# Softmax over rows of 512: VectorE's and ScalarE's work in blocks of eight rows in place of four

## The chip, the cores and the metric

The kernel runs on one core of one Trainium2 chip. The metric is the device time of one execution in microseconds (us), as the median over several runs. The kernel before the change took 163.42 us (median of 10 runs, 162.94 to 163.77).

Four engines of the core appear in this kernel. VectorE (DVE in the profile) and ScalarE (ACT) compute. SyncE (SP) only starts loads. GpSimd (POOL) writes four constants at the start and does nothing else. Beside them, sixteen DMA engines move data between the HBM (the chip's main memory) and the SBUF (the core's working memory of 128 partitions). Each engine runs its own list of instructions in order, and waits on semaphores where it needs another engine's result or a transfer.

## The reference

The input is 16 x 1024 rows of 512 float32 numbers, 33.55 MB. Every row is divided by 0.5, and the softmax is taken over it:

```python
temp = 0.5
x_scaled = x / temp
x_max = np.max(x_scaled, axis=-1, keepdims=True)
exp_x = np.exp(x_scaled - x_max)
return (exp_x / np.sum(exp_x, axis=-1, keepdims=True)).astype(np.float32)
```

The output has the size of the input, so 67.1 MB have to be moved in all.

## The kernel before

The 16384 rows are cut into eight tiles of 2048 rows. Each of the 128 partitions holds G = 16 consecutive rows of a tile, which is 32 KB a partition and 4 MB a tile. The pool of tiles has six buffers (`data`, `bufs=6`), and the whole computation is done in place: a tile is loaded, each row in it is replaced by its exponentials and then by the scaled result, and the tile is stored from where it lies. So the loads of the first six tiles wait for nothing, and the loads of tiles 6 and 7 wait until tiles 0 and 1 have been stored.

A tile is loaded with one DMA, issued by SyncE (line 59); only tile 0 is loaded in two, its first four rows and then its other twelve, so that the work can begin early. A tile is stored with one DMA of 4 MB, issued from ScalarE's instruction list (line 102).

The computation goes by blocks of B = 4 rows a partition, so four blocks a tile and 32 in all. Four functions handle a block:

- `shift` runs on VectorE. One reduction (line 65) takes the negated maximum of all four rows of the block, and one small multiplication (line 67) doubles it, because the input's scaling by 1 / 0.5 is folded into the exponential. The result is called `bias`.
- `exponentials` runs on ScalarE. One instruction a row (line 74) computes exp(2x + bias) and its sum over the row. In the trace it shows as two entries, the activation and a short reading of the accumulator.
- `scale_vector` runs on VectorE. One reciprocal of the block's sums (line 87), and then one multiplication a row for three of the four rows (line 89).
- `scale_scalar` runs on ScalarE: the fourth row is multiplied by its reciprocal there, with one copy instruction with a scale (line 95).

The order on every engine is written out by hand in a loop over the blocks (lines 104 to 116). Iteration i issues, in this order, the load of a tile (when block i is the first of one), `shift(i)` and `exponentials(i)`, then `scale_vector(i - 1)`, `scale_scalar(i - 2)` and `store(i - 3)`. A store is issued only when block i - 3 was the last of its tile. So the store of a tile stands on ScalarE's list three blocks behind the tile's last one: behind the exponentials of the third block of the next tile, and behind one scaled copy. For the last tile, the three iterations after the last block finish what is left.

The words "iteration" and "block" are used in this sense below; a block is written (tile, first row), so (7, 8) is the third block of the last tile.

Of the kernel before, what the change touches and what calls it, by code (L numbers as in the profile page):

```python
# [1 line left out]

# [4 lines left out]


@with_exitstack
def kernel(  # L10
    ctx: ExitStack,
    tc: tile.TileContext,
    x: bass.AP,
    out: bass.AP,
):
    nc = tc.nc
    fp32 = mybir.dt.float32
    P = nc.NUM_PARTITIONS
    AX = mybir.AxisListType.X
    EXP = mybir.ActivationFunctionType.Exp  # L20
    COPY = mybir.ActivationFunctionType.Copy
    MAX = mybir.AluOpType.max

    D = x.shape[-1]
    xf = x.flatten_outer_dims()
    of = out.flatten_outer_dims()
    N = xf.shape[0]

    G = 16
    B = 4
    N_ACT = 1
    C = N // (P * G)
    assert C * P * G == N
    xr = xf.rearrange("(c p g) d -> c p g d", p=P, g=G)
    outr = of.rearrange("(c p g) d -> c p g d", p=P, g=G)

    FIRST = [(0, 4), (4, 16)]  # L40

    data = ctx.enter_context(tc.tile_pool(name="data", bufs=6))
    stats = ctx.enter_context(tc.tile_pool(name="stats", bufs=6))

    ctx.enter_context(tc.manual_schedule())


    warm = stats.tile([P, 1], fp32, name="warm", bufs=1)
    nc.vector.memset(warm, 0.0)  # L49
    nc.scalar.activation(out=warm, in_=warm, func=EXP)  # L50

    tiles = {}
    blocks = [(c, b) for c in range(C) for b in range(0, G, B)]
    state = {}

    def load(c):
        xt = tiles[c] = data.tile([P, G, D], fp32, name="xt")
        for lo, hi in FIRST if c == 0 else [(0, G)]:
            nc.sync.dma_start(out=xt[:, lo:hi, :], in_=xr[c][:, lo:hi, :])  # L59

    def shift(i):
        c, b = blocks[i]
        xb = tiles[c][:, b : b + B, :]
        negmax = stats.tile([P, B], fp32, name="negmax")
        nc.vector.tensor_reduce(negmax, xb, axis=AX, op=MAX, negate=True)  # L65
        bias = stats.tile([P, B], fp32, name="bias")
        nc.vector.tensor_scalar_mul(bias, negmax, 2.0)  # L67
        state[i] = (xb, bias)

    def exponentials(i):  # L70
        xb, bias = state[i]
        sums = stats.tile([P, B], fp32, name="sums")
        for g in range(B):
            nc.scalar.activation(  # L74
                out=xb[:, g, :],
                in_=xb[:, g, :],
                func=EXP,
                bias=bias[:, g : g + 1],
                scale=2.0,
                accum_out=sums[:, g : g + 1],  # L80
            )
        state[i] = (xb, sums)

    def scale_vector(i):
        xb, sums = state[i]
        recip = stats.tile([P, B], fp32, name="recip")
        nc.vector.reciprocal(recip, sums)  # L87
        for g in range(B - N_ACT):
            nc.vector.tensor_scalar_mul(xb[:, g, :], xb[:, g, :], recip[:, g : g + 1])  # L89
        state[i] = (xb, recip)  # L90

    def scale_scalar(i):
        xb, recip = state[i]
        for g in range(B - N_ACT, B):
            nc.scalar.activation(  # L95
                out=xb[:, g, :], in_=xb[:, g, :], func=COPY, scale=recip[:, g : g + 1]
            )

    def store(i):
        c, b = blocks[i]  # L100
        if b + B == G:
            nc.scalar.dma_start(out=outr[c], in_=tiles[c])

    n = len(blocks)
    for i in range(n + 3):
        if i < n:
            if blocks[i][1] == 0:
                load(blocks[i][0])
            shift(i)
            exponentials(i)  # L110
        if 1 <= i <= n:
            scale_vector(i - 1)
        if 2 <= i <= n + 1:
            scale_scalar(i - 2)
        if 3 <= i:
            store(i - 3)


# [1 line left out]
_INS = ['x']  # L120
_OUTS = [((16, 1024, 512), 'float32')]


# [23 lines left out]
```

## Time and profile before

| what | value |
|---|---|
| median of 10 runs | 163.42 us |
| the profiled execution's own time | 163.34 us |
| span from its first to its last instruction | 161.4 us |
| VectorE busy | 119.7 us, 74% of the span |
| ScalarE busy | 114.8 us, 71% of the span |
| moved by DMA | 67.14 MB, 416 GB/s over the span |

The profiled execution's time is 1.94 us longer than its span; that difference lies outside of what the instructions show. The profile calls an instruction by its line and by the tile that it writes and reads. In a line of the timeline, the first two numbers are the start and the duration in us, and the bracket at the end tells how long the engine had been idle and what ended that. The names ACTq and SPq stand for the sequencers of ScalarE and SyncE, which issue DMAs without keeping the engine itself busy. In the table of windows, the columns are the window and its length, then the busy time and the number of instructions of each engine, the clock of TensorE (which is not used here), the share of time that the DMA engines were busy, and the data rate in GB/s.

### The profile page before, as it was taken

The numbers are of one execution on the slowest core, as the hardware profiler recorded it, in microseconds if no ns is written. First come the engines' busy times: TensorE is split into PE (matmuls) and PEld (weight loads), VectorE is DVE, ScalarE is ACT, GpSimd is POOL, SyncE is SP. The second block draws the span as 40 slices with busy tenths as digits, with TensorE's granted clock in tenths as the row PEclk, the third lists the DMA queues.
The fourth block names the chain that finished last, engine by engine and source line by source line (L and its number), as shares of the span: only waits on it lengthen the run. The fifth ranks groups of instructions, "written<-read, shape, count | busy, mean of one in ns | idle before, by whom it ended". The sixth has DMA issues, their size and how long they took to land.

```text
span 161.4 us, 563 instructions
## 1 busy us (share of the span) xinstructions
DVE 119.7 (74%) x193; ACT 114.8 (71%) x290; POOL 0.2 (0%) x4
## 2 busy tenths in 40 slices
DVE  0608999999999999999994999369991899830000
ACT  3072799999999998999995799809996299970000
POOL 0000000000000000000000000000000000000000
DMA  5999999999999999999999999999999999999991
GB/s 183 467 455 455 390 455 455 392 455 317 424 463 406 430 463 406 422 471 406 422 463 400 439 463 398 439 455 406 439 455 406 439 455 408 430 455 414 430 455 57
DMA packets 2452, 67.14 MB, mean 416 GB/s; under 512 B 272, under 2 KB 272, under 8 KB 272
## 3 DMA queue, kind: packets, MB, share of 16 engines
q1 hardware_dynamic: 1296, 33.56, 49.2%
q10 hardware_dynamic: 1152, 33.55, 48.2%
q14 instruction: 4, 0.03, 0.0%
HBM read 33.55 MB, written 33.55 MB: 416 GB/s over the span
## 4 chain that ended last, share of the span: by engine, by line
DVE 47%; DMA 36%; ACT 5%; issue 1%; SPq 0%
DMA xt<-in_x_dram 36%; DVE negmax L65 29%; DVE xt L89 15%; ACT xt L74 4%; DVE bias L67 2%; ACT xt L95 1%; DVE recip L87 1%; SPq L59 0%
## 5 line engine op out<-in xcount | busy, mean ns | idle before, releaser
L74 ACT ACTIVATE xt<-xt,bias 128x512 f32<-128x512 f32 x128 | 90.8, 710 | 28.7 <-DVE bias L67 28.7
L65 DVE TENSOR_REDUCE negmax<-xt 128x4 f32<-128x2048 f32 x32 | 73.0, 2281 | 19.6 <-DMA xt<-in_x_dram 19.6
L89 DVE TENSOR_SCALAR xt<-xt,recip 128x512 f32<-128x512 f32 x96 | 40.9, 483 | 1.1
L74 ACT ACTIVATION_READ_ACCUMULATOR xt<-xt,bias 128x1 f32 x128 | 23.9, 187 | 0.0
L95 ACT ACTIVATE xt<-xt,recip 128x512 f32<-128x512 f32 x32 | 22.4, 706 | 0.0
L87 DVE RECIPROCAL recip<-sums 128x4 f32<-128x4 f32 x32 | 5.5, 171 | 1.6 <-ACT xt L74 1.6
L67 DVE TENSOR_SCALAR bias<-negmax 128x4 f32<-128x4 f32 x32 | 5.4, 170 | 1.1
L50 ACT ACT_TABLE_LOAD x1 | 1.3, 1283 | 0.7 <-PEq L131 0.7
L49 DVE MEMSET warm<- 128x1 f32 x1 | 0.1, 59 | 0.8 <-PEq L131 0.8
L50 ACT ACTIVATE warm<-warm 128x1 f32<-128x1 f32 x1 | 0.2, 203 | 0.0
L131 POOL MEMSET const-bfloat16-1.0<- 128x1 bf16 x1 | 0.1, 101 | 0.0
L131 POOL MEMSET const-uint8-127<- 128x1 uint8 x1 | 0.1, 101 | 0.0
L131 POOL MEMSET const-float32-0.0<- 128x1 f32 x1 | 0.1, 98 | 0.2 <-issue 0.2
L131 POOL MEMSET const-float32-1.0<- 128x1 f32 x1 | 0.1, 98 | 0.0
## 6 DMA issues: line engine op xcount, KB each, us to landing
out_dram<-xt ACTq DMA_DIRECT2D x8, 4096.0 KB, 27.0
xt<-in_x_dram SPq DMA_DIRECT2D x7, 4096.0 KB, 46.8
xt<-in_x_dram SPq DMA_DIRECT2D x1, 3072.0 KB, 11.6
xt<-in_x_dram SPq DMA_DIRECT2D x1, 1024.0 KB, 4.7
```

The source lines that it names most:

```text
L49: nc.vector.memset(warm, 0.0)
L50: nc.scalar.activation(out=warm, in_=warm, func=EXP)
L65: nc.vector.tensor_reduce(negmax, xb, axis=AX, op=MAX, negate=True)
L67: nc.vector.tensor_scalar_mul(bias, negmax, 2.0)
L74: nc.scalar.activation(out=xb[:, g, :], in_=xb[:, g, :], func=EXP, bias=bias[:, g : g + 1], scale=2.0, accum_out=sums[:, g : g + 1],)
L87: nc.vector.reciprocal(recip, sums)
L89: nc.vector.tensor_scalar_mul(xb[:, g, :], xb[:, g, :], recip[:, g : g + 1])
L95: nc.scalar.activation(out=xb[:, g, :], in_=xb[:, g, :], func=COPY, scale=recip[:, g : g + 1])
L131: nc = _bacc.Bacc("TRN2", target_bir_lowering=False, num_devices=1)
```

## The change

The block is eight rows in place of four, so two blocks a tile. Tile 0 begins with two blocks of four rows, for the first of which the separate small load provides the data, and then has one block of eight. There are 17 blocks in place of 32. The loop over the blocks and the order within an iteration are left as they are, and so are the loads and the buffers.

An instruction that handled a whole block (maximum, doubling, reciprocal) now handles eight rows, and there are 17 of each in place of 32. The instructions that handle a row are as many as before: two rows of eight (one of four) are scaled on ScalarE, by `B // 4`, and the others on VectorE. Since the store of a tile still stands three blocks behind the tile's last block, it now stands behind the exponentials of the first block of the tile after the next: iteration i = (c + 2, 0) issues the store of tile c.

```diff
     G = 16
-    B = 4
-    N_ACT = 1
...
     FIRST = [(0, 4), (4, 16)]
+    BLOCKS_FIRST = [(0, 4), (4, 4), (8, 8)]
+    BLOCKS = [(0, 8), (8, 8)]
...
-    blocks = [(c, b) for c in range(C) for b in range(0, G, B)]
+    blocks = [(c, b, B) for c in range(C) for b, B in (BLOCKS if c else BLOCKS_FIRST)]
...
     def shift(i):
-        c, b = blocks[i]
+        c, b, B = blocks[i]
         xb = tiles[c][:, b : b + B, :]
-        negmax = stats.tile([P, B], fp32, name="negmax")
-        nc.vector.tensor_reduce(negmax, xb, axis=AX, op=MAX, negate=True)
-        bias = stats.tile([P, B], fp32, name="bias")
-        nc.vector.tensor_scalar_mul(bias, negmax, 2.0)
+        negmax = stats.tile([P, 8], fp32, name="negmax")
+        nc.vector.tensor_reduce(negmax[:, 0:B], xb, axis=AX, op=MAX, negate=True)
+        bias = stats.tile([P, 8], fp32, name="bias")
+        nc.vector.tensor_scalar_mul(bias[:, 0:B], negmax[:, 0:B], 2.0)
         state[i] = (xb, bias)
 
     def exponentials(i):
+        B = blocks[i][2]
         xb, bias = state[i]
-        sums = stats.tile([P, B], fp32, name="sums")
+        sums = stats.tile([P, 8], fp32, name="sums")
         for g in range(B):
...
     def scale_vector(i):
+        B = blocks[i][2]
         xb, sums = state[i]
-        recip = stats.tile([P, B], fp32, name="recip")
-        nc.vector.reciprocal(recip, sums)
-        for g in range(B - N_ACT):
+        recip = stats.tile([P, 8], fp32, name="recip")
+        nc.vector.reciprocal(recip[:, 0:B], sums[:, 0:B])
+        for g in range(B - B // 4):
             nc.vector.tensor_scalar_mul(xb[:, g, :], xb[:, g, :], recip[:, g : g + 1])
         state[i] = (xb, recip)
 
     def scale_scalar(i):
+        B = blocks[i][2]
         xb, recip = state[i]
-        for g in range(B - N_ACT, B):
+        for g in range(B - B // 4, B):
...
     def store(i):
-        c, b = blocks[i]
+        c, b, B = blocks[i]
         if b + B == G:
             nc.scalar.dma_start(out=outr[c], in_=tiles[c])
```

## The prediction

> **What bounds the kernel now.** I read the page from the top: engine busy times, the slices, the queues, the chain. They contradict each other at first.
>
> ```profile
> DVE 119.7 (74%) x193; ACT 114.8 (71%) x290; POOL 0.2 (0%) x4
> ...
> DMA  5999999999999999999999999999999999999991
> ...
> q1 hardware_dynamic: 1296, 33.56, 49.2%
> q10 hardware_dynamic: 1152, 33.55, 48.2%
> ...
> DVE 47%; DMA 36%; ACT 5%; issue 1%; SPq 0%
> ```
>
> The chain gives VectorE 47%, so it looks like the bound. But the DMA row is 9 in every slice between the first and the last, and the two queues (q1 loads, q10 stores) fill 97.4% of the sixteen engines' span between them. A chain follows one way back through the waits, and it can pass through an engine that is merely always occupied. So I cut the span into five windows, by what the queues do in them.
>
> ```profile
> 2.00:34.00 32.00, 23.33 (x33) 20.23 (x54) 0.00 (x0) 1.00 1.01 432
> 34.00:40.00 6.00, 5.86 (x13) 5.50 (x15) 0.00 (x0) 1.00 1.04 382
> 40.00:122.00 82.00, 74.03 (x120) 70.74 (x181) 0.00 (x0) 1.00 1.00 432
> 126.00:156.00 30.00, 16.02 (x28) 15.39 (x38) 0.00 (x0) 1.00 1.01 435
> 156.00:161.40 5.40, 0.00 (x0) 0.00 (x0) 0.00 (x0) 1.00 0.32 140
> ```
>
> Loads alone run at 432 GB/s, loads and stores together at 432, stores alone at 435; only the window in which the stores begin is lower (382). 67.1 MB at 432 GB/s are 155.3 us of the 161.4. The rest is the way to the first packet (1.71 us in the trace's packet records), those 0.7 us at the mixing (6 x 50 / 432), and an uneven end: the sixteen parts of the last store land between 158.45 and 160.53, eleven of them by 158.8. The DMA engines bound the kernel. The waits say the same (columns: us in total, times, longest):
>
> ```profile
> DVE negmax L65 <- DMA xt<-in_x_dram: 19.6, 5, 4.8
> ```
>
> and so does the timeline at the last tile's arrival:
>
> ```profile
> 125.59 2.29 DVE L65 TENSOR_REDUCE negmax<-xt 128x4 f32<-128x2048 f32 x1 [4.10 <-DMA xt<-in_x_dram]
> ```
>
> VectorE stands idle for data before tiles 5, 6 and 7 too. After the last load there are 18.7 us of computing to the last store's issue at 144.28, and 16.2 us more to its landing, of which its 4.19 MB take 9.65 at 435 GB/s: for about 6 us it waits behind the store of tile 6.
>
> **The change part by part: VectorE's work.** Rows of one block in steady state:
>
> ```profile
> 16.57 2.28 DVE L65 TENSOR_REDUCE negmax<-xt 128x4 f32<-128x2048 f32 x1
> ...
> 18.89 0.17 DVE L67 TENSOR_SCALAR bias<-negmax 128x4 f32<-128x4 f32 x1
> 18.96 0.17 DVE L87 RECIPROCAL recip<-sums 128x4 f32<-128x4 f32 x1
> ...
> 19.17 1.28 DVE L89 TENSOR_SCALAR xt<-xt,recip 128x512 f32<-128x512 f32 x3
> ...
> 20.36 2.28 DVE L65 TENSOR_REDUCE negmax<-xt 128x4 f32<-128x2048 f32 x1
> ```
>
> From start to start a block of four takes 2.32 + 0.07 + 0.21 + 1.19 = 3.79 us. For eight rows no row exists. The doubling of four numbers lasts 0.17 us and is nearly all start-up, so four more rows add 2.28 - 0.17 = 2.11 us at least and 2.28 at most. I take 2.11: 4.43 + 0.07 + 0.21 + 6 x 0.40 = 7.1 us (7.3 at most) against 7.58 for two blocks of four. That removes 15 reductions' start-ups, doublings and reciprocals, 15 x 0.51 = 7.7 us of busy time. All of it lies beside DMA work and buys nothing; without that cover it would be a gain of about 15 x 0.48 = 7.2 us. ScalarE needs 10 x 0.705 = 7.05 us for eight rows, so neither engine gets behind the DMA's 19.4 us a tile (8.39 MB at 432 GB/s).
>
> **The stores move.** The issue for tile c moves from the third block of tile c + 1 to the first block of tile c + 2. Tile 0: VectorE's reductions start at 16.57, 22.5, 29.6 and, for (2, 0), 36.7; its bias is ready 4.6 us later, so the store is issued at 41.3, not 34.28: 7.0 us later (7.7 with the dear reduction). On ScalarE's list ten computing instructions, not five, stand between that bias and the DMA. Before, this was the passage:
>
> ```profile
> 34.25 0.72 ACT L74 ACTIVATE xt<-xt,bias 128x512 f32<-128x512 f32 x1 [0.25 <-DVE bias L67]
> 34.28 0.38 ACTq L102 DMA_DIRECT2D out_dram<-xt  x1
> ```
>
> The sequencer passed five for 0.03 us. With ten it costs between 0 and 6.4 us (nine starts of 0.705); I take 0, the value of the five.
>
> [...]
>
> A later store leaves the DMA engines to the loads for as long. In mixed flow each queue gets half (a 4 MB load takes 19.4 us there, tile 6 to tile 7), so 7 us of loads alone in place of half speed bring each later load 7 us forward: tiles 5, 6 and 7 land at 80, 99.2 and 118.6, not 87.1, 106.2 and 125.6. What the loads gain the stores lose, and the end of all bytes stays. That holds while either queue always has work. SyncE waits for stores 0 and 1 before it issues loads 6 and 7: they land at 66 and 86 (59.2 and 78.8 before, plus 7), while loads 5 and 6 still run to 80 and 99. Stores 1 to 5 are issued at 55, 70, 85, 104 and 123, each 8 us or more before the store ahead of it is through (66, 86, 106, 125, 131). GpSimd has nothing in its list.
>
> **The tail is the close place.** The store of tile 6 is now issued in iteration 17, behind all exponentials, and it needs the copies of (6, 8), which stand behind the exponentials of (7, 8). From the last landing at 118.6: second reduction at 125.7, bias at 130.3, eight exponentials 5.65 us, two copies 1.3 us: issue at 137.3, or 18.7 us after the landing. Before it was 135.72. Its packets began at 138.76 by the trace's records, right behind those of store 5, and this turn is unchanged. Queued behind its wait on ScalarE are the copies of (7, 8) and the last store, which is issued at about 139.7 and whose turn comes at 148. From issue to first packet the trace has two prices: 0.98 us for the first load on empty queues (0.73 to 1.71) and 3.89 us for the first store amid loads (34.28 to 38.17). I take 0.98, since no loads run then: first packet possible at 138.3, 0.5 us early, cost 0. By the other end it is 141.2: the early engines idle 2.4 us, their last parts land at up to 161.1 in place of 160.53, cost 0.6 us. If the two copies of (7, 0), which stand just ahead of it in the list, hold it up too, 1.2 us more.
>
> [...] VectorE is at 74% here. [...]
>
> **The sum:** 0 for VectorE, 0 for the moved stores, 0 in the tail. The profiled execution took 163.34 us, span 161.4 and 1.94 around it; the median is 0.08 higher. I forecast 163.4. Within 0.2% means 0.33 us, about what a measurement of this kernel tells from no change.
>
> **The rivals.**
> - Store 6 comes late (slower). For it: a margin of 0.5 us only, and the 3.89 us row. Against it: the engines that would wait are those that finish about 2 us before the last. It decides once the issue takes over 3.6 us to its first packet (an idle time of 2.1 us takes the early engines' 158.8 to 160.9, 0.33 past 160.53); price 0.6, up to 1.8 us: 164.0 to 165.2.
> - The lag among the DMA engines changes. The last of them is 2.1 us behind the first at the end, and the packets slow down where the stores begin. Half of it gone gives 162.4, half as much again 164.4; nothing in the trace says which.
> - VectorE was the bound after all, as the chain's 47% suggests: 163.4 - 7.2 = 156.2. Against it: its 19.6 us of waits for data.
> - The later stores simply end later, because the loads do not use the time: 163.4 + 7.0 = 170.4. Against it: 432 GB/s with loads alone.
>
> **How the numbers follow.** No change 0.60; store 6 late 0.15; the lag 0.18, of it 0.10 faster and 0.08 slower; VectorE 0.04; stores simply later 0.03. Faster 0.10 + 0.04 = 0.14, slower 0.15 + 0.08 + 0.03 = 0.26, same 0.60. The range runs from half the smaller lag, 162.8, to 164.4, which takes in the first price of the late store and the larger lag; VectorE's gain, the 7 us, half of the late store's longer prices and a bit of the lag are left out.
>
> **What would show it.** Right: first store at 41 to 48, VectorE's wait for tile 7 ending 7 us or more earlier, 17 reductions of 4.4 us, three main windows still at 432 to 435 GB/s, and the same last landing. Wrong: a slice below 9 between 130 and 145, a store issued after the one ahead of it has landed, or a rate that depends on the mix of loads and stores.

## The result and the profile after

The changed kernel takes 162.61 us (median of 9 runs, 162.26 to 163.09), against 163.37 us for the kernel before (median of 32). The ratio is 0.9957, with a 95% interval of 0.9946 to 0.9967. It was measured three more times in the experiments: 0.9942, 0.9963 and 0.9953. So the change saves about 0.7 us, where no change was forecast. The profiled execution of the changed kernel took 162.99 us (span 161.2), so it is one of the slower ones and shows only half of the gain.

The page of the changed kernel, by the same parts as shown before (busy times, DMA slices, the third queue, the chain):

```profile
DVE 114.0 (71%) x148; ACT 113.1 (70%) x290; POOL 0.2 (0%) x4
...
DMA  5999999999999999999999999999999999999991
...
q14 instruction: 3, 0.02, 0.0%
...
DMA 44%; DVE 34%; ACT 7%; issue 1%; SPq 0%
```

The DMA engines are still busy from end to end. The chain has changed its face (VectorE 34% in place of 47%), and that means as little as before. The windows of the changed kernel, cut where its stores begin and its loads end:

```profile
2.00:34.00 32.00, 23.52 (x24) 18.68 (x52) 0.00 (x0) 1.00 1.02 436
34.00:48.00 14.00, 13.87 (x18) 13.60 (x36) 0.00 (x0) 1.00 0.98 396
48.00:115.00 67.00, 59.65 (x81) 61.84 (x162) 0.00 (x0) 1.00 1.00 433
118.00:156.00 38.00, 15.76 (x25) 16.40 (x40) 0.00 (x0) 1.00 1.01 436
```

Loads alone, both together, stores alone: 436, 433, 436 GB/s. The rate does not depend on the mix, and a dip remains where the stores begin (396 over 14 us; the same window of the kernel before gives 398). For the middle one of the sixteen DMA engines, nothing has been gained: the median of the last store's sixteen landings is at 158.66 us before and at 158.69 after.

What differs is how late the last of the sixteen is: 1.86 us behind that median before, 1.61 us in this profile of the changed kernel, and 0.95, 0.69 and 0.87 us in the three profiles of it taken later, which lie nearer to its usual time (162.35, 162.20 and 162.38 us). I call this distance the **lag** below.

Every run has its span on record too, and so the part of its time that lies outside of the span. In the three later measurements of the changed kernel the span is 0.55 to 0.75 us shorter, in the mean of the runs, than that of the kernel before beside it. The part outside is shorter as well, by 0.07 to 0.16 us (1.85 or 1.86 us, against 1.93 to 2.01). So about 0.1 us of the gain lies outside of what the instructions show.

The line that moves with it is one that the prediction did not quote. It is the queue that the page calls instruction. The experiments show that its fetches go with the length of the engines' lists: two with 61 entries on VectorE's in the program, nine with 750 memsets more on GpSimd's. On the page of the kernel before:

```profile
q14 instruction: 4, 0.03, 0.0%
```

Four fetches of 8,192 bytes while the kernel runs; three after the change. In the packet records of before they start at 31.5, 43.2, 85.9 and 136.3 us. At 43.2 and 136.3 VectorE is at the 54th and the 186th entry of its list in the trace, 132 entries apart (the trace counts waits and other entries that the page leaves out, 201 in all before the change where the page has 193). The changed kernel's list has 156 entries and never gets there; its fetches are at 31.5, 54.1 and 83.2, and at 54.1 VectorE is again at its 54th entry. The other two go with ScalarE's list: it is at the 53rd and the 190th entry at 31.5 and 85.9 us before, and at the 51st and the 189th at 31.5 and 83.2 us after. From here a fetch of this kind is called a refill. The queues of both kernels in the stretch from 126 to 140 us, before:

```profile
q10 hardware_dynamic: 212, 5.96, 98.9%
q14 instruction: 1, 0.01, 0.1%
```

and after:

```profile
q10 hardware_dynamic: 215, 6.06, 100.4%
```

The refills are carried by the same sixteen DMA engines as the data. I strung the packet records together to one chain for each DMA engine, from the end of a packet to the next start. In both kernels, the two that carry refills are the last to finish: at 159.95 and 160.18 us before, and at 159.70 and 159.97 after, while the other fourteen end between 158.0 and 159.1. A refill's packet lasts 0.31 us, and the data packet behind it is longer than usual (at 136.6 us before the change 1.56 us in place of 1.21; 1.32 to 1.75 behind the seven refills of the two profiles), so that a refill sets its engine back by 0.4 to 0.9 us.

In the profile of before, though, the refill at 136.3 us is not on the last of the two. The chain that ends at 160.18 carries the one at 85.9, which remains after the change, and the chain that ends at 159.95 carries the one at 136.3. The landings say the same: from the store whose median landing is at 129.6 us to the next, at 139.3, the second latest of the sixteen falls back from 0.97 to 1.75 us behind the median, and the latest stays at 1.92. In this one execution, then, the fourth refill did not set the end.

The price of a refill in the time of the kernel comes from the runs that follow.

### The profile page after: what moved, and what is told of

Same layout as the page of the kernel before. It is cut to its first block, busy times and chain, and to the rows that moved or that the text cites. A ratio compares the mean times of both kernels' runs of the same rounds, so it can differ in the third digit from the quotient of the medians.

```text
span 161.2 us, 517 instructions
## 1 busy us (share of the span) xinstructions
DVE 114.0 (71%) x148; ACT 113.1 (70%) x290; POOL 0.2 (0%) x4
## 4 chain that ended last, share of the span: by engine, by line
DMA 44%; DVE 34%; ACT 7%; issue 1%; SPq 0%
DMA xt<-in_x_dram 25%; DVE negmax L65 23%; DMA out_dram<-xt 19%; DVE xt L91 9%; ACT xt L75 5%; ACT xt L98 2%; DVE bias L67 1%; DVE recip L89 0%; SPq L59 0%
## 5 line engine op out<-in xcount | busy, mean ns | idle before, releaser
L65 DVE TENSOR_REDUCE negmax<-xt 128x8 f32<-128x4096 f32 (+1 forms) x17 | 70.8, 4163 | 18.0 <-DMA xt<-in_x_dram 18.0
L91 DVE TENSOR_SCALAR xt<-xt,recip 128x512 f32<-128x512 f32 x96 | 39.5, 481 | 0.6
L98 ACT ACTIVATE xt<-xt,recip 128x512 f32<-128x512 f32 x32 | 21.0, 706 | 0.0
L89 DVE RECIPROCAL recip<-sums 128x8 f32<-128x8 f32 (+1 forms) x17 | 3.3, 193 | 3.2 <-ACT xt L75 3.2
L67 DVE TENSOR_SCALAR bias<-negmax 128x8 f32<-128x8 f32 (+1 forms) x17 | 2.9, 171 | 0.6
```

Of the source, the lines that this page charges most:

```text
L65: nc.vector.tensor_reduce(negmax[:, 0:B], xb, axis=AX, op=MAX, negate=True)
L67: nc.vector.tensor_scalar_mul(bias[:, 0:B], negmax[:, 0:B], 2.0)
L89: nc.vector.reciprocal(recip[:, 0:B], sums[:, 0:B])
L98: nc.scalar.activation(out=xb[:, g, :], in_=xb[:, g, :], func=COPY, scale=recip[:, g : g + 1])
```

## The experiments

Three theories were set against each other. **L**: VectorE's shorter list saves a refill, and with it lag of the last DMA engine. **S**: the gain comes from the stores that begin later. **W**: it comes from VectorE's 5.7 us less work.

**The long list given back (two runs).** The changed kernel with 45 tiny memsets on VectorE, which bring its list to the old length:

```diff
+    pad = stats.tile([P, 1], fp32, name="pad", bufs=1)
...
         state[i] = (xb, recip)
+        if i < 15:
+            for _ in range(3):
+                nc.vector.memset(pad, 0.0)
```

> The changed kernel with 45 one-element memsets (59 ns each in the profile of before) added on VectorE, three in each of the first 15 iterations, so that VectorE's list is as long as before the change (201 entries in the trace, the changed kernel 156). Nothing else is altered. Theory L (length of the list): the change gained because VectorE's shorter list needs one refill less; the trace of before has an 8 KB instruction fetch at 136.3 us, when VectorE is at its 186th entry, which costs one DMA engine 0.65 us near the end, and the trace after has none there. L expects the fetch to come back and the time to return to 163.3 to 163.4 (ratio to before 1.000). Theory S (stores): the gain comes from the stores that begin 7 to 10 us later. S expects 162.6, ratio 0.9955. Theory W (work): it comes from VectorE's 5.7 us less busy time; the memsets give back 2.7 us of it, so about 163.0.

> The changed kernel with 45 one-element memsets on VectorE once more, beside the changed kernel. The first gave 0.9985. L: 0.4 us over the changed kernel beside it, 0.998 to 0.999, with four fetches. W: half of VectorE's work is back, 0.998 as well; this run tells L from W only together with the one that adds the work without the entries.

The first gave 0.9985 (0.9971 to 0.9999), the second 0.9994 (0.9981 to 1.0007). The second ran beside the changed kernel (0.9953), so by the ratios 0.67 us of its gain of 0.77 were gone, and by the medians 0.53 of 0.71. Inside of the span all of it was gone: the spans of the two runs are 0.09 and 0.08 us shorter than those of the kernel before, which is less than the runs resolve, and the second's is 0.61 us longer than the changed kernel's beside it. What remained lies outside of the span. The profile of the second, busy times and the fetches:

```profile
DVE 116.2 (72%) x193; ACT 113.1 (70%) x290; POOL 0.2 (0%) x4
...
q14 instruction: 4, 0.03, 0.0%
```

The fourth refill is back, at 132.4 us, and the lag rises across it from 0.82 us (store landing at 131) to 1.21 us (the next one, at 141). In the first run the lag rises from 0.66 to 1.36 us across the refill at 132.8. What L says of the list holds; but half of VectorE's work came back as well (116.2 us of 114.0 to 119.7), so W was not yet out.

**The work without the entries.**

```diff
+    pad = stats.tile([P, 384], fp32, name="pad", bufs=1)
...
         state[i] = (xb, recip)
+        if i < 15:
+            nc.vector.memset(pad, 0.0)
```

> The changed kernel with one memset of 384 elements a partition on VectorE in each of the first 15 iterations: about 0.3 to 0.45 us each, 4.5 to 6.8 us of work, about as much as the change took off VectorE (5.7 us), but with 15 list entries more only, so that the list stays under the place of the second refill. W (the gain is VectorE's shorter work) expects the gain to go, 0.999 to 1.000 of before. L expects it to stay: the ratio of the changed kernel beside it, about 0.996, and three instruction fetches in the trace.

It gave 0.9950 (0.9935 to 0.9965), the same as the changed kernel beside it (0.9953). The profile, busy times, fetches and the added line:

```profile
DVE 118.9 (74%) x163; ACT 113.1 (70%) x290; POOL 0.2 (0%) x4
...
q14 instruction: 3, 0.02, 0.0%
...
L96 DVE MEMSET pad<- 128x384 f32 x15 | 5.7, 378 | 0.4
```

VectorE is as busy as before the change to within 0.8 us, there are three refills, and the whole gain is kept. VectorE's pace is also that of the run with the tiny memsets: a block of eight takes 7.50 us here, 7.40 there and 7.14 in the changed kernel. The two versions differ in 30 entries of the list, and in the gain. W is out.

**The changed kernel beside the others (three runs).** These are references; the first is

> The changed kernel as it is, once more, as the reference for the runs beside it: 0.9957 of before, with an interval of about 0.001 to each side. Of the sixteen DMA engines, the two that fetch instructions should again be the last to finish, about 1.5 us behind the others.

and the others

> The changed kernel again as the reference for the three beside it: 0.9942 to 0.9957 of before.

> The changed kernel as the reference for the runs beside it: 0.994 to 0.9965 of before. Its last landing minus the median of the sixteen should be 0.7 to 1.6 us, as in three profiles so far, where the four profiles with four refills had 1.3 to 2.0.

They gave 0.9942 (0.9929 to 0.9955), 0.9963 (0.9951 to 0.9975) and 0.9953 (0.9938 to 0.9968). The lag was 0.95, 0.69 and 0.87 us, below the 1.5 us that I expected in the first.

**A shorter list with blocks of four.** The kernel before, without the doubling (line 67):

```diff
-        bias = stats.tile([P, B], fp32, name="bias")
-        nc.vector.tensor_scalar_mul(bias, negmax, 2.0)
-        state[i] = (xb, bias)
+        state[i] = (xb, negmax)
```

> The kernel before without the 32 doublings: the exponential takes the negated maximum itself as its bias, exp(2x - max), which the division by the sum cancels; blocks of four and the place of the stores stay. VectorE's list has 32 entries less (about 169, under the place of the second refill). L expects the late fetch to be gone and the time to fall to about 162.6 (0.9955). S expects 163.4 (1.000), since the stores still begin at about 33 to 34 us. W expects 32 x 0.17 = 5.4 us less busy time to do what the change did, also 162.6.

0.9978 (0.9967 to 0.9989): three refills (30.2, 48.7 and 85.0 us) and a lag of 1.01 us. One edit that has nothing to do with blocks takes the fourth refill away and gives half of the change's gain (the span is 0.41 us shorter than before's; the part outside is not). That it gives only half was expected by none of the three.

**The stores moved.** The changed kernel with its stores about 7 us earlier, twice:

```diff
-    for i in range(n + 3):
+    for i in range(n + 2):
...
             shift(i)
+        if 2 <= i:
+            store(i - 2)
+        if i < n:
             exponentials(i)
         if 1 <= i <= n:
             scale_vector(i - 1)
-        if 2 <= i <= n + 1:
-            scale_scalar(i - 2)
-        if 3 <= i:
-            store(i - 3)
+            scale_scalar(i - 1)
```

> The changed kernel with the stores issued about 7 us earlier, as before the change: the store of block i - 2 stands ahead of the exponentials of block i, and the copies of a block directly behind the exponentials of the next. Blocks of eight and VectorE's list stay. The first store should be issued at about 34.5 us. S expects the gain to go, 163.4 (1.000). L expects 162.6 (0.9955), except that ScalarE's list grows by seven waits to 325 instructions in the program, and if that brings ScalarE a third refill, up to 0.7 us of the gain are lost with it, which the trace's instruction fetches would show. W expects 162.6.

> The changed kernel with its stores 7 us earlier, a second time, now beside the changed kernel itself. The first gave 0.9965 (0.9953 to 0.9978). If the stores' place is worth 0.0015 and the list's length the rest, 0.0015 above the changed kernel's ratio; L alone expects the same ratio as the changed kernel, S alone 1.000.

The first store was issued at 34.4 us. The ratios were 0.9965 (0.9953 to 0.9978) and 0.9963 (0.9952 to 0.9975), the second the same as the changed kernel beside it (0.9963). ScalarE's list got no third refill before the last store had ended. S alone is out: the stores are back at their old place, and the gain is there. By the spans it is smaller, 0.33 and 0.38 us, where the changed kernel beside the second has 0.55; the difference of 0.17 us is about what the runs resolve.

The kernel before with its stores two blocks later, twice:

```diff
-    for i in range(n + 3):
+    for i in range(n + 5):
...
-        if 3 <= i:
-            store(i - 3)
+        if 5 <= i:
+            store(i - 5)
```

> The kernel before with the stores issued two blocks of four later (five blocks behind the last of their tile in place of three), which puts the first store at about 41.9 us where the changed kernel has it. Blocks of four and VectorE's list of 201 stay. S expects the whole gain, 162.6 (0.9955). L and W expect 163.4 (1.000).

> The kernel before with its stores two blocks later, a second time, because the first gave 0.9984 (0.9969 to 0.9998), which lies between S's 0.9955 and L's 1.000. If the stores' place gives a part of the gain, 0.998 to 0.999 again; if that was chance, 1.000.

0.9984 (0.9969 to 0.9998) and 0.9987 (0.9974 to 1.0001), with the first store at 41.8 us, four refills, and lags of 2.03 and 1.87 us. So late stores seem to be worth 0.2 us on the kernel before. The spans show where: they are only 0.07 and 0.04 us shorter than those of the kernel before, which is less than the runs resolve, and the part outside of the span is 0.13 and 0.16 us shorter. With four refills, late stores gain nothing inside of the span.

The part outside goes with one more instruction fetch. In the four profiles in which a fetch starts 1.7 us or more behind the last instruction (before, no doubling, added work, and the version with no refill on VectorE below), 1.94 us or more of the time lies outside of the span; in all others it is 1.85 us or less. No run tests whether that fetch is the cause.

Stores one block of eight later still:

```diff
-    for i in range(n + 3):
+    for i in range(n + 4):
...
-        if 3 <= i:
-            store(i - 3)
+        if 4 <= i:
+            store(i - 4)
```

> The changed kernel with its stores one block of eight later still (four blocks behind the last of their tile in place of three), so that the first is issued at about 48.4 us. VectorE's list stays. If later stores are worth 0.0015 for each 7 us, as the runs with the late stores on the kernel before suggest (0.9984 and 0.9987), this gives 0.9935 beside the changed kernel's 0.995. If the stores' place is worth nothing, 0.995. If the tail is too tight now, with store 6 issued behind all copies, a stretch without DMA work near 139 us and up to 1 us more than the changed kernel.

0.9975 (0.9959 to 0.9991), beside 0.9963 for the changed kernel. The two intervals overlap, so the time alone does not show a loss; the span is 0.3 us longer than the changed kernel's in the mean of the runs, and the profile shows the third case of the expectation, one store earlier than I had it. The window from 128 to 134 us of this run:

```profile
128.00:134.00 6.00, 2.75 (x9) 6.00 (x17) 0.00 (x0) 1.00 0.91 388
```

and of the changed kernel:

```profile
128.00:134.00 6.00, 3.17 (x9) 5.84 (x16) 0.00 (x0) 1.00 0.99 426
```

The store of tile 5 is issued at 129.4 us, and the one ahead of it has then nearly drained. The DMA engines pause, and here all sixteen land within 0.26 us of each other afterwards: lag 0.18, but the median at 159.84. So the place where later stores bring a stall lies one block beyond the change.

**Refills of an engine that does nothing else.** Memsets on GpSimd, first 900, then 750:

```diff
+    for _ in range(900):
+        nc.gpsimd.memset(pad, 0.0)
```

> The changed kernel with 900 one-element memsets put on GpSimd, which is otherwise idle. Nothing waits for them, and they should run in the first 100 us or so. GpSimd's list needs seven more 8 KB refills. Theory L (a refill costs the DMA engine that brings it 0.6 to 0.9 us, and the last DMA engine sets the end): the seven cost one engine 7 x 0.65 = 4.6 us. If it is one of the fourteen engines that had no refills, it ends at 158.3 + 4.6 = 162.9 where the last one ended at 160.0, so about +2.9 us over the changed kernel, 165.5; if it is one of the two that serve ScalarE and VectorE, up to +4.6, 167.2. Theories S (the stores' place) and W (VectorE's work): no change from the changed kernel, 162.6.

> As the run with 900 memsets on GpSimd, but 750 of them, because there GpSimd itself ran until the end (0.18 us a memset, 165 us) and hid what was to be seen. At that pace the 750 end at about 140 us, and GpSimd's list needs six more refills. With 900, the last DMA packet of the profile ended at 160.8 us, against 159.3 to 160.0 in two profiles of the changed kernel, and four DMA engines were late in place of two, so the refills seem to be shared between two further engines. L: three or four refills of 0.65 us on one engine, 158.3 + 1.95 to 2.6 = 160.3 to 160.9 for its last packet: 0.3 to 1.0 us over the changed kernel beside it, ratio to before 0.997 to 1.002. S and W: no change, 0.995.

The first gave 167.49 us, 1.0257 (1.0244 to 1.0270), but GpSimd itself ran to the end of the span, so the time is not the DMA's alone; the lag was 3.92 us. The second gave 164.94 us, 1.0100 (1.0084 to 1.0116), against 162.59 for the changed kernel beside it. Its fetches, and GpSimd's last work:

```profile
q14 instruction: 9, 0.07, 0.1%
```

```profile
138.98 0.88 POOL L54 MEMSET pad<- 128x1 f32 x6
```

GpSimd is done at 140 us, and nothing waits for it. The last store's median landing is at 158.60, as ever, and the lag is 3.51 us, 2.6 to 2.8 us more than in the kernel's later profiles without the memsets. Six refills cost 2.35 us of the time. The chains of this run show one DMA engine that carries all six of them (at 11.1, 34.4, 58.9, 83.7, 106.1 and 130.9 us) and sends its last packet until 161.7 us, while the other fifteen end by 159.8. So each refill set this engine back by 0.6 us. I had expected 0.3 to 1.0 us in all, because I took the refills to be shared between two engines; the direction is L's, and S and W had expected nothing. Here the path from refill to time is plain to see: one engine late by its refills, the others as ever.

**A third refill on VectorE.** 14 tiny memsets in each iteration:

```diff
+        if i < 15:
+            for _ in range(14):
+                nc.vector.memset(pad, 0.0)
```

> The changed kernel with 14 one-element memsets in each of the first 15 iterations on VectorE (210 in all): VectorE's list passes the places of the second and of a third refill, three in all where the changed kernel has one. L: two more refills, 1.3 us on the engine that serves VectorE, which ended 0.3 us before the last: about +1.0 us over the changed kernel, 163.6, above the kernel before. W: 210 x 0.06 = 12.6 us of work more than the changed kernel, twice what the change removed, so about 164.3 if work counts as it did in the change, but also slower stores by 3 us. S: 162.6 or a little less, since the stores come later still.

175.25 us, 1.0727 (1.0713 to 1.0742), far beyond all three theories. The memsets of a row start 0.125 us apart, not 0.06, so a block of eight took 8.8 us, the stores came late, and the DMA engines stood still:

```profile
131.00:139.00 8.00, 7.52 (x17) 6.20 (x17) 0.00 (x0) 1.00 0.05 22
```

From 131 to 139 us they move 22 GB/s. The run says nothing on refills; it shows how near VectorE is to being the bound: a block of eight may take 7.1 or 7.5 us (the run with the added work), but not 8.8.

**A version with no refill on VectorE.**

```diff
-    FIRST = [(0, 4), (4, 16)]
-    BLOCKS_FIRST = [(0, 4), (4, 4), (8, 8)]
+    FIRST = [(0, 8), (8, 16)]
+    BLOCKS_FIRST = [(0, 8), (8, 8)]
...
-        bias = stats.tile([P, 8], fp32, name="bias")
-        nc.vector.tensor_scalar_mul(bias[:, 0:B], negmax[:, 0:B], 2.0)
-        state[i] = (xb, bias)
+        state[i] = (xb, negmax)
...
-        for g in range(B - B // 4):
-            nc.vector.tensor_scalar_mul(xb[:, g, :], xb[:, g, :], recip[:, g : g + 1])
+        V = B - B // 4
+        nc.vector.tensor_tensor(
+            out=xb[:, 0:V, :], in0=xb[:, 0:V, :],
+            in1=recip[:, 0:V].unsqueeze(2).to_broadcast([P, V, D]),
+            op=mybir.AluOpType.mult,
+        )
```

> A version that follows from L: the changed kernel with VectorE's list so short (61 entries in the program) that it needs no refill in the run. The doubling goes (the bias is the negated maximum itself, which the division cancels; it overflows for rows whose maximum is about 88 or more, which these inputs are far from), the six scalings of a block become one multiplication by a broadcast reciprocal, and tile 0 has two blocks of eight. ScalarE keeps its two refills. L: two fetches in the trace, a lag of the last DMA engine of 0.6 to 1.2 us, and 162.1 to 162.5, ratio 0.993 to 0.995, 0 to 0.5 us under the changed kernel. W, by VectorE's work: the broadcast multiplication is dearer or cheaper than six scalings by an amount that no row shows, so no number. A later first store (block of eight first) costs nothing by L.

162.54 us, 0.9956 (0.9939 to 0.9973), the same as the changed kernel beside it (162.46 us, 0.9953), and not the 0 to 0.5 us less that L had expected. Busy times, fetches and the new multiplication:

```profile
DVE 125.3 (78%) x49; ACT 112.9 (70%) x290; POOL 0.2 (0%) x4
...
q14 instruction: 2, 0.02, 0.0%
...
L89 DVE TENSOR_TENSOR xt<-xt,recip 128x3072 f32<-128x3072 f32 x16 | 53.7, 3358 | 0.5
```

Two refills are left, both ScalarE's, and the lag is 0.64 us, hardly less than with three (0.69 to 0.95 in the references). The chains give a reason: in all four profiles of the changed kernel the last engine is the one with ScalarE's two refills, and the one with VectorE's is second. Here too the engine with ScalarE's two is the last. Nothing shows that any version beat the changed kernel.

The profiles together, with refills counted up to the end of the last store. Left out are the stores one block later still (three refills, lag 0.18) and the 14 memsets in each iteration (lag 0.10), where the DMA engines stood still and the late ones caught up:

| refills | kernels | lag of the last DMA engine (us) | mean |
|---|---|---|---|
| 2 | no refill on VectorE | 0.64 | |
| 3 | changed kernel (four profiles) | 1.61, 0.95, 0.69, 0.87 | 1.03 |
| 3 | no doubling; early stores (two); added work | 1.01; 1.60, 1.06; 0.71 | 1.10 |
| 4 | before; late stores (two); long list (two) | 1.86; 2.03, 1.87; 1.31, 1.15 | 1.64 |
| 9 and 10 | memsets on GpSimd | 3.51 and 3.92 | |

From three to four refills the mean rises by 0.6 us (1.06 over the eight profiles with three), but the two groups overlap: 0.69 to 1.61 and 1.15 to 2.03. Nor is all of the 0.6 us the fourth refill's own doing. Across it the lag rises by 0.8 us (one profile with late stores), 0.7 and 0.4 (the long list), and not at all in the profile of before and in the other one with late stores, where the engine with ScalarE's refills was later still. The mean of the five is 0.4 us.

The times and spans of all runs are the firmer ground. Every version with four refills is at 0.9984 of before or above, with a span at most 0.09 us shorter. Every one with two or three is at 0.9978 or below, with a span 0.24 to 0.81 us shorter.

## Why the prediction was wrong

Forecast was no change, 163.4 us (162.8 to 164.4); it became 162.61 and lies 0.2 us under the range.

- **What bounds the kernel: right.** The DMA engines are busy throughout, at the same rate in every mix (433 to 436 GB/s outside of the stretch in which the stores begin), and 5.7 us less work on VectorE bought nothing (shown by the run that adds the work back).
- **VectorE's costs: right in the block's time, and beside the point.** The reduction over eight rows lasts 4.41 us, where 2.28 + 2.11 = 4.39 was taken. A block of eight takes 7.14 us from start to start (7.15 in the lines below, 116.87 to 124.02), where 7.1 was forecast. The busy time fell by 5.7 us and not by the forecast 7.7. Of the 17 reductions 15 are over eight rows and two over four, so the sign "17 reductions of 4.4 us" could not come.
- **The moved stores: right.** Lines of the changed kernel's timeline:

```profile
41.37 0.72 ACT L75 ACTIVATE xt<-xt,bias 128x512 f32<-128x512 f32 x1 [0.16 <-DVE bias L67]
...
43.62 0.37 ACTq L105 DMA_DIRECT2D out_dram<-xt  x1
...
116.87 4.42 DVE L65 TENSOR_REDUCE negmax<-xt 128x8 f32<-128x4096 f32 x1 [4.99 <-DMA xt<-in_x_dram]
...
124.02 4.41 DVE L65 TENSOR_REDUCE negmax<-xt 128x8 f32<-128x4096 f32 x1
...
135.67 0.34 ACTq L105 DMA_DIRECT2D out_dram<-xt  x1
```

The bias that releases the first store came at 41.4 us (forecast 41.3), but the DMA followed 2.25 us later, when three of the ten instructions ahead of it were through and the fourth had started. I had taken 0 out of 0 to 6.4, the value of the five, which the sequencer had passed in 0.03 us. The delay moved nothing at the end: tile 7 landed 8.7 us earlier, and no stall came.
- **The tail: right.** The store of tile 6 was issued 18.8 us after the last landing (18.7 forecast), at 135.67, and its packets followed those of store 5. That this is a close place is shown by the run with stores one block later, whose stall came at the store before.
- **The sum: here it failed.** "All of it lies beside DMA work and buys nothing" priced 45 list entries fewer by their time on VectorE alone. The term that is missing is the list itself: with the entries given back, 0.61 us of the span came back, and 0.53 us (by the medians) to 0.67 us (by the ratios) of the time, beside the changed kernel; with the work given back in 15 entries, nothing did. The page had the row (four instruction fetches). I stepped over it because its share is 0.0%. A share is a mean over sixteen engines, and the run with 750 memsets shows that one of them with refills can set the end.
- **The rivals.** "The lag among the DMA engines changes" is the one that came nearest: the profiles of the changed kernel have a lag of 1.03 us in the mean, that of before 1.86. Half of it gone was priced at 162.4, given 0.10, with the words that nothing in the trace says which. The trace pointed to a reason, since the two late engines carry all the refills; it did not give the size, since the latest engine's refills were not those that the change removes. The other rivals were wrong: no late store 6, no gain through VectorE's time, no 7 us.
- **The range.** Half of the smaller lag's gain of 1.0 us would have put its lower end at 162.9 and not at 162.8; the result lies under both.
- **Grouping on an engine with time to spare.** VectorE was at 74% before the change and its time bought nothing; grouping helped all the same, by the number of instructions (the 45 entries given back took 0.53 to 0.67 us with them). The idle time of the DMA engines in the tail, priced at up to 0.6 us, did not come.

Two things remain open. The first is how the list's refill comes to cost 0.5 to 0.7 us: the lags explain about 0.4 us of it in the mean, and in the profile of before none. The second is why three runs with three refills gain only 0.33 to 0.41 us of span (no doubling, and the early stores twice; their first store is issued at 33.0 to 34.5 us), where the changed kernel, the added work and the version with no refill on VectorE (first store at 43.6 to 45.1 us) gain 0.55 to 0.81. So the stores' place may count once the fourth refill is gone; no run shows it beyond noise.

## What to carry to other kernels

In this kernel, bound by DMA, the end was set by the slowest of the DMA engines and not by their mean (with the 750 memsets by one that ended at 161.7 us, where the other fifteen had ended by 159.8). In another one like it, compare the median and the last of the final transfer's landings before calling an edit free. The instruction lists were fetched here through the same DMA engines as the data, 8,192 bytes at a time. Past a refill's place, 45 entries more on VectorE's list cost 0.53 to 0.67 us, and six refills more cost 2.35 us, even on an engine that is idle otherwise (GpSimd); so count the instruction fetches on the page. A rate of 432 to 435 GB/s in the main windows of the kernel before still left about half a us that went with one refill.

## What the runs showed of the hardware

- A refill is 8,192 bytes, its packet 0.31 us, and it sets its DMA engine back by 0.4 to 0.9 us; the data packet behind it is longer, 1.32 to 1.75 us in the profiles of before and after in place of the usual 1.21.
- Six further refills, by an engine that no other one waits for, cost 2.35 us (162.59 to 164.94). All six were carried by one DMA engine.
- The DMA rate was the same within 1% with loads alone, with stores alone and mixed (436, 436 and 433 GB/s); only where the stores began was it lower (398 GB/s over 14 us before, 396 after, or 1.2 to 1.3 us of work).
- A tiny memset shows 0.06 us on VectorE, but fourteen in a row started 0.125 us apart.
- The time outside of the span was 1.94 us or more in the four profiles with an instruction fetch 1.7 us or more behind the last instruction, and 1.85 us or less in the others.
